# A pooling mixer's running sums in four pieces each, and the memory queries' weights in the mixer's own tiles

## The chip, the cores and the metric

The kernel runs on one core of one Trainium2 chip. A core has a matrix engine (PE, TensorE), three engines that work on vectors (DVE is VectorE, ACT is ScalarE, POOL is GpSimd) and a queue that issues transfers (SP, SyncE). Each engine takes its own instructions strictly in the order in which they stand in its queue, and waits by itself for what an instruction needs. The metric is the device time of one execution in microseconds (us); the time of a kernel is the median of its runs.

## What is computed

The reference is one layer of a hybrid encoder for 1088 tokens (1024 of a prompt and 64 of a sample), width 1024. One normalized input h is projected into the columns of three branches and three gates; the branches are joined by their gates, and a gated feed-forward block follows. Two parts matter here.

```python
h = rmsnorm(x, g_mix)
p = h @ w_in                 # split into qa, ka, va, qi, ki, wi, ub, qm, gates
...
# branch B, the pooling mixer: 4 channel groups of 128 columns of ub,
# for group g the mean of the last 2, 4, 8 or 16 frames, minus the frame,
# then a 128 x 128 map per group and a scale per channel
...
# branch M: the memory queries
qm = rmsnorm(qm.reshape(B, T, N_HEADS_M, HD_M), g_qm)
```

Branch A picks for every query the keys with the highest scores. The kernel finds the cut by halving an integer interval bit by bit, and this search runs through the whole stretch that is looked at here.

## The kernel before, in words

All products are of fp32 values, each held as a rounded high part and the rest (`round_hi`, line 96, on GpSimd here; `lo_of`, line 86, on DVE). `matmul3` (lines 115 to 122) makes three TensorE products of each pair: high by high, high by low, low by high. The normalized input stands transposed in `hh` and `hl`, 8 blocks of 128 rows by 1088 tokens. Tokens are cut into 3 chunks of 364, 362 and 362 columns (`CH`), or into 9 blocks of up to 128 (`TS`).

**The pooling mixer** (pool `pp`) goes over four groups with windows 2, 4, 8 and 16. For each, `wblock` loads 128 columns of weights and splits them into `uhi` and `ulo`; 72 products give the group's 1088 columns; ACT copies them into the tile `e` (lines 470 and 472). GpSimd then makes the running sums (line 485): the first add joins each column with its neighbour, the second adds pairs at distance 2, and so on, so that a window of 2, 4, 8, 16 needs 1, 2, 3, 4 adds, 10 in all, each over up to 1117 columns, into one of the two tiles `pw`. DVE mends the first 16 columns (lines 487 and 488), scales the sum and subtracts the frame (line 489), and ACT and DVE split the result into `ph` and `pl` (line 494 and line 86). `pooled`, the map of a group (9 products, ACT `bh`, DVE `bl`, lines 455 and 456), stands one group later; that of the last group stands in the loop of the memory queries, at block 4.

**The memory queries** (pool `qm`, after the pooling mixer's) load the weights of each half (256 columns) as two pieces of four blocks of 128 rows each, split them into `tmhi` and `tmlo`, make 24 products for each of 9 token blocks (`token_major`), normalize (`head_norm`) and store. The pool `qm` is opened when `pp` is closed and lies in the same place of the on-chip memory, so what is written first there waits for the last readers of the tiles of `pp`.

**What sets the order.** The program is written stage by stage, but a scheduler that simulates a timeline puts each engine's instructions into their final order. So that TensorE has something to do where a stage waits, it puts in products of the gates ("fill work": tile `fl`, ACT's sigmoid `fsg` at line 237, weights `whi` and `wlo` from `fraw`; later also the branches' output products with `fpt`, a load of a stored gate, at line 598, which DVE multiplies in at line 601). The three PSUM buffers of `fl` come free when ACT has made `fsg`.

**The search** runs at the same time on ACT and DVE. In one round, ACT counts for three blocks of queries (line 817, `junk_a`) and DVE for five in four instructions (line 820, `junk_v`), how many scores lie above the candidate. DVE then compares the counts with the cut (`hit_a`, `hit_v`, line 836), sets the bit (`tbit_a`, `tbit_v`, line 837) and makes the next candidate (`cand_a`, `cand_v`, line 834). The next round's counts on ACT wait for `cand_a`, those on DVE for `cand_v`.

Of the kernel before, what the change touches and what calls it, by code (L numbers as in the profile page):

```python
# [9 lines left out]
F32R = mybir.dt.float32r  # L10
AF = mybir.ActivationFunctionType
OP = mybir.AluOpType
# [33 lines left out]
def encoder_step(ctx: ExitStack, tc: tile.TileContext, a: dict, o: list):  # L46
# [38 lines left out]
    def lo_of(lo, src, hi):  # L85
        return V.tensor_tensor(lo, src, hi.bitcast(F32), op=OP.subtract)  # L86
# [70 lines left out]
    def token_major(w, b, n_out):  # L157
        t0, n = TS[b]
        ps = mm()[:n, :n_out]
        matmul3(ps, [(hh[:, k, t0:t0 + n], hl[:, k, t0:t0 + n], w[0][:, k], w[1][:, k]) for k in range(KT)])  # L160
        return ps

    def tm_weights(pool, src, n, bufs=1):
        hi = pool.tile([128, KT, n], F32R, name="tmhi", tag="tmhi", bufs=bufs)
        lo = pool.tile([128, KT, n], F32R, name="tmlo", tag="tmlo", bufs=bufs)
        step = 1024 // n
        for k0 in range(0, KT, step):
            k1 = min(KT, k0 + step)
            raw = wp.tile([128, 1024], F32, name="raw", tag="raw", bufs=3)[:, :(k1 - k0) * n]
            raw = raw.rearrange("p (k j) -> p k j", j=n)  # L170
            SP.dma_start(raw, src[:, k0:k1])
            round_hi(hi[:, k0:k1], raw)
            lo_of(lo[:, k0:k1], raw, hi[:, k0:k1])
        return hi, lo

    def chunks_of(n):
        return [(0, n)] if n <= 512 else [(0, n // 2), (n // 2, n // 2)]
# [215 lines left out]
    with tc.tile_pool(name="mem", bufs=1) as mp:  # L393
        gmem = mp.tile([128, D], F32, name="gmem")
        bcast_row(gmem, a["g_mem"], 0, D)
        gkm = mp.tile([128, 128], F32, name="gkm")
        bcast_row(gkm, a["g_km"], 0, 128)
        mh = mp.tile([128, KT, 256], F32R, name="mh")
        ml = mp.tile([128, KT, 256], F32R, name="ml")
        for i in range(2):  # L400
            xt = raw_tile()
            SP.dma_start(xt, a["mem_prompt"][i * 128:(i + 1) * 128])
            h = row_norm(mp, xt, 128, gmem)
            transpose_split(h, 128, mh[:, :, i * 128:(i + 1) * 128], ml[:, :, i * 128:(i + 1) * 128])
        for c in range(4):
            w = tm_weights(mp, a["w_mem_kv"][c], 256)
            for i in range(2):
                ts = slice(i * 128, (i + 1) * 128)
                ps = mm()[:, :256]
                matmul3(ps, [(mh[:, k, ts], ml[:, k, ts], w[0][:, k], w[1][:, k]) for k in range(KT)])  # L410
                cs = slice((c % 2) * 256, (c % 2) * 256 + 256)
                kv = mp.tile([128, 2, 128], F32, name="kv", tag="kv", bufs=2)
                kf = kv.rearrange("p h d -> p (h d)")
                if c < 2:
                    head_norm(mp, ps, 128, 2, 128, kv)
                    V.tensor_tensor(kv, kv, gkm[:, None, :].to_broadcast([128, 2, 128]), op=OP.mult)
                    SP.dma_start(o[6][ts, cs], kf)
                    SP.dma_start(mem_k[ts, cs], kf)
                else:
                    A.copy(kf, ps)  # L420
                    SP.dma_start(o[7][ts, cs], kf)
                    SP.dma_start(mem_v[ts, cs], kf)
# [6 lines left out]
    if True:  # L429
        W0 = 15 + SEQ + 15  # L430
        E_ = W0 + DEC
        phl_c = tc.tile_pool(name="phl", bufs=1)
        phl = phl_c.__enter__()
        pwh = phl.tile([128, 4, 128], F32R, name="pwh")
        pwl = phl.tile([128, 4, 128], F32R, name="pwl")
        with tc.tile_pool(name="pool", bufs=1) as pp:
            fix = pp.tile([128, 4, 16], F32, name="fix")
            SP.dma_start(fix, bass.AP(tensor=a["fix"].tensor, offset=a["fix"].offset, ap=[[0, 128], [16, 4], [1, 16]]))
            hist = raw_tile()
# [18 lines left out]

            wait = []
            for g, win in enumerate(WINDOWS):  # L460
                wts = [pp.tile([128, 1024], F32R, name=nm, tag=nm, bufs=1) for nm in ("uhi", "ulo")]
                wh, wlo = wblock(a["w_ub"][g], (KT, 128), None, wts)
                e = pp.tile([128, E_], F32, name="e", tag="e", bufs=1)
                V.memset(e[:, 0:15], 0.0)
                G.tensor_scalar(e[:, 15 + SEQ:W0], hc[:, g], 1.0, 1.0, op0=OP.mult, op1=OP.mult)
# [16 lines left out]
                cur, step = e, 1  # L482
                while step < win:
                    nxt = pp.tile([128, E_], F32, name="pw", tag="pw", bufs=2)
                    G.tensor_tensor(nxt[:, 2 * step - 1:], cur[:, 2 * step - 1:], cur[:, step - 1:E_ - step], op=OP.add)
                    cur, step = nxt, 2 * step
                V.tensor_tensor(cur[:, 15:31], cur[:, 15:31], fix[:, g], op=OP.mult)
                V.tensor_tensor(cur[:, 15:31], cur[:, 15:31], e[:, 15:31], op=OP.subtract)
# [8 lines left out]

    with tc.tile_pool(name="qm", bufs=1) as tp:
        for half in range(2):
            w = tm_weights(tp, a["w_qm"][half], 256)  # L500
            for b in range(NB):
                if half == 0 and b == 4:
                    pooled(*wait.pop())
                t0, n = TS[b]
                ps = token_major(w, b, 256)
                qn = tp.tile([128, 2, 128], F32, name="qn", tag="qn", bufs=2)
                head_norm(tp, ps, n, 2, 128, qn[:n])
                SP.dma_start(q_m[t0:t0 + n, half * 256:(half + 1) * 256], qn[:n].rearrange("p h d -> p (h d)"))

    phl_c.__exit__(None, None, None)  # L510


# [998 lines left out]
```

## Time and profile before

| | us |
|---|---|
| median of 3 runs | 1746.39 (1741.99 to 1746.84) |
| the profiled execution's own time | 1744.31 |
| its span, first to last instruction | 1742.5 |
| PE busy with products | 1696.9 (97% of the span) |
| DVE busy | 1178.9 |
| ACT busy | 811.5 |
| POOL busy | 408.5 |

The rows below come from one profiled execution. In a row of a timeline the first number is the start in us from the span's start, the second the time from the first to the last of the instructions joined in it; in brackets, where it stands, is the idle time of the engine just before and what ended it. The granted clock of TensorE is given as a share of its full level.

### The profile page before, as it was taken

How to read it: one execution, taken by the hardware profiler on the slowest of the kernel's cores; microseconds unless marked ns; L12 is line 12 of the kernel's file. 1: busy time of each engine (PE TensorE's matmuls, PEld its weight loads, DVE VectorE, ACT ScalarE, POOL GpSimd, SP SyncE). 2: the span in 40 equal slices, each digit the busy share in tenths (PEclk: the TensorE clock that was granted, in tenths of full speed). 3: DMA queues.
4: the chain of work that ended last, by engine and by line, in shares of the span. 5: the costliest groups of instructions: out<-in, count | busy, mean ns of one | idle time of the engine just before them, and what ended most of it. 6: DMA issues, size and time to landing. Idle time of an engine off the chain costs nothing.

```text
span 1742.5 us, 32497 instructions
## 1 busy us (share of the span) xinstructions
PE 1696.9 (97%) x12088; PEld 1642.4 (94%) x12088; DVE 1178.9 (68%) x2602; ACT 811.5 (47%) x1951; POOL 408.5 (23%) x444
## 2 busy tenths in 40 slices
PE   8999999999999999999999999999999999999999
PEld 7999999899999999877798998999999999999999
DVE  7566999999964443689874688556658656465553
ACT  5457576646632442469732343334434333353431
POOL 4201323345421122675302442000101000000000
PEclk9999999999999999999999999999999999999999
DMA  6122541222366334760273326543445443498661
GB/s 231 59 68 64 170 137 46 80 72 91 118 204 194 99 107 140 259 193 4 77 258 119 112 80 214 177 150 106 174 153 186 142 144 136 133 341 266 208 194 52
DMA packets 147263, 250.86 MB, mean 144 GB/s; under 512 B 16920, under 2 KB 93328, under 8 KB 147104
## 3 DMA queue, kind: packets, MB, share of 16 engines
q1 hardware_dynamic: 147104, 248.78, 43.8%
q8 instruction: 95, 1.56, 0.4%
q14 instruction: 64, 0.52, 0.1%
HBM read 173.63 MB, written 75.09 MB: 143 GB/s over the span
## 4 chain that ended last, share of the span: by engine, by line
PE 59%; DVE 6%; DMA 3%; issue 2%; ACT 2%; POOL 1%; SPq 0%; DVEq 0%; POOLq 0%; ACTq 0%
PE mm L1169 24%; PE mm L1392 13%; PE mm L122 10%; PE fl L122 7%; PE acc L973 1%; DVE lo L86 1%; PE tr L943 1%; PE mm L966 1%; DVE wlo L86 1%; DVE fr L1123 1%; DMA side_a<-gt 1%; DMA gt<-side_m 1%; DVE pl L86 1%; DMA fpt<-gate_b 1%; DMA side_m<-fpt 0%
## 5 line engine op out<-in xcount | busy, mean ns | idle before, releaser
L1169 PE MATMUL mm<-hi,whi 128*128 128x288 f32 (+1 forms) x1120 | 323.0, 289 | 2.3 <-ACT whi L1161 2.3
L1169 PE MATMUL mm<-hi,wlo 128*128 128x288 f32 (+1 forms) x1120 | 323.5, 290 | 0.2
L1169 PE MATMUL mm<-lo,whi 128*128 128x288 f32 (+1 forms) x1120 | 323.4, 289 | 0.0
L1169 PEld LDWEIGHTS mm<-hi,whi 128*128 128x128 f32 x1120 | 211.8, 189 | 3.0 <-ACT whi L1161 3.0
L1169 PEld LDWEIGHTS mm<-lo,whi 128*128 128x128 f32 x1120 | 211.8, 189 | 0.0
L1169 PEld LDWEIGHTS mm<-hi,wlo 128*128 128x128 f32 x1120 | 211.0, 189 | 0.6 <-DVE wlo L86 0.6
L122 PE MATMUL fl<-hh,whi 128*128 128x362 f32 (+1 forms) x576 | 191.1, 332 | 4.5 <-DVE fpt L601 2.3
L122 PE MATMUL fl<-hl,whi 128*128 128x362 f32 (+1 forms) x576 | 190.8, 331 | 0.1
L122 PE MATMUL fl<-hh,wlo 128*128 128x362 f32 (+1 forms) x576 | 188.5, 331 | 0.0
L1392 PE MATMUL mm<-ul,wh 128*128 128x256 f32 (+1 forms) x600 | 171.7, 288 | 0.0
L1392 PE MATMUL mm<-uh,wh 128*128 128x256 f32 (+1 forms) x600 | 171.2, 288 | 0.0
L1392 PE MATMUL mm<-uh,wl 128*128 128x256 f32 (+1 forms) x600 | 170.3, 288 | 0.0
L122 PE MATMUL mm<-tmhi,hh 128*128 128x256 f32 (+3 forms) x432 | 122.2, 288 | 2.7 <-POOL tmhi L96 2.7
L122 PE MATMUL mm<-tmlo,hh 128*128 128x256 f32 (+3 forms) x432 | 123.0, 286 | 0.6 <-DVE tmlo L86 0.6
L122 PE MATMUL mm<-tmhi,hl 128*128 128x256 f32 (+3 forms) x432 | 122.3, 285 | 0.0
L86 DVE TENSOR_TENSOR wlo<-raw,whi 128x1024 fp32r<-128x1024 f32 (+1 forms) x76 | 77.4, 1030 | 58.8 <-ACT whi L1161 38.3
L817 ACT ACTIVATE junk_a<-score,cand_a,sgn_a 128x512 f16<-128x512 f32 (+2 forms) x93 | 95.5, 1027 | 43.3 <-DVE cand_a L834 32.3
L122 PEld LDWEIGHTS fl<-hh,whi 128*128 128x128 f32 x576 | 109.0, 189 | 6.3 <-issue 2.5
L1392 PEld LDWEIGHTS mm<-ul,wh 128*128 128x128 f32 x600 | 112.7, 188 | 0.0
L1392 PEld LDWEIGHTS mm<-uh,wh 128*128 128x128 f32 x600 | 112.4, 188 | 0.0
L1392 PEld LDWEIGHTS mm<-uh,wl 128*128 128x128 f32 x600 | 112.2, 188 | 0.0
L122 PEld LDWEIGHTS fl<-hl,whi 128*128 128x128 f32 x576 | 109.0, 189 | 0.9 <-DVE hl L86 0.4
(404 smaller groups left out, 4565.1 us busy)
## 6 DMA issues: line engine op xcount, KB each, us to landing
uf<-u SPq DMA_DIRECT2D x75, 272.0 KB, 4.5
raw<-in_w_up_dram SPq DMA_DIRECT2D x26, 512.0 KB, 4.0
fraw<-in_w_gates_dram SPq DMA_DIRECT2D x23, 512.0 KB, 3.8
fr<-in_w_gate_dram SPq DMA_DIRECT2D x22, 512.0 KB, 4.3
dr<-in_w_down_dram SPq DMA_DIRECT2D x22, 512.0 KB, 5.8
s<-dr SPq DMA_DIRECT2D x22, 512.0 KB, 3.2
raw<-s SPq DMA_DIRECT2D x44, 256.0 KB, 3.6
side<-side_a SPq DMA_DIRECT2D x8, 1088.0 KB, 7.4
```

The costliest lines, as they stand in the source:

```text
L86: return V.tensor_tensor(lo, src, hi.bitcast(F32), op=OP.subtract)
L122: PE.matmul(ps, l, r, start=i == 0, stop=i == len(prods) - 1)
L817: A.activation(junk[:n, :nk], sc, AF.Sign, bias=bj, scale=1.0 if scale is None else scale[:n, j:j + 1], accum_out=sj)
L943: PE.matmul(lg[:n, i * 512:i * 512 + cn], qT[:, h, :n], kT[:, kv, s, k0 + c:k0 + c + cn], start=s == 0, stop=s == 1)
L966: PE.transpose(pt[:cn, i * n:(i + 1) * n], probs[i][:, c:c + cn], ident[:n, :n])
L973: PE.matmul(acc, vv, r, start=ji == 0 and i == 0, stop=ji == nj - 1 and i == 1)
L1123: V.scalar_tensor_tensor(hb[e][:, :n], ys[i][:, kk], gffn_c[:, kk:kk + 1], rb[:, :n], op0=OP.mult, op1=OP.mult)
L1169: PE.matmul(dst[i], l, r, start=start and j == 0, stop=stop and j == 11, skip_group_check=True)
L1392: PE.matmul(acc[f, i], l[:, fs], r[:, cs], start=start and j == 0, stop=stop and j == 2, skip_group_check=True)
```

## The change

It has two parts.

**The running sums** are cut by columns into pieces of 280 (`PIECE`): four instructions instead of one for each add, 40 instead of 10 on GpSimd. What is computed is the same.

**The weights of the memory queries** no longer go to a pool of their own. The pool `pp` stays open until the memory queries are done. Its two weight tiles `uhi` and `ulo` become two halves of one tile of 2048 columns (tag `ub`). The high part of a half's weights (`qmhi`) takes that tile, and the low part takes the two tiles of the running sums (tag `pw`, 1117 columns each, of which 1024 are used): blocks 0 to 3 in one, blocks 4 to 7 in the other. `token_major` reads the low part as a list of eight blocks. Other callers of `tm_weights` keep `tmhi` and `tmlo`.

```diff
-    def tm_weights(pool, src, n, bufs=1):
-        hi = pool.tile([128, KT, n], F32R, name="tmhi", tag="tmhi", bufs=bufs)
-        lo = pool.tile([128, KT, n], F32R, name="tmlo", tag="tmlo", bufs=bufs)
+    def tm_weights(pool, src, n, given=None):
+        if given:
+            hi, lo = given
+        else:
+            hi, lo = [pool.tile([128, KT, n], F32R, name=nm, tag=nm, bufs=1) for nm in ("tmhi", "tmlo")]
+            lo_all, lo = lo, [lo[:, k] for k in range(KT)]
...
             round_hi(hi[:, k0:k1], raw)
-            lo_of(lo[:, k0:k1], raw, hi[:, k0:k1])
-        return hi, lo
+            if given:
+                lo_of(lo[k0 // step], raw, hi[:, k0:k1])
+            else:
+                lo_of(lo_all[:, k0:k1], raw, hi[:, k0:k1])
+        return hi, [l[:, k] for l in lo for k in range(l.shape[1])] if given else lo
...
-        with tc.tile_pool(name="pool", bufs=1) as pp:
+        pp_c = tc.tile_pool(name="pool", bufs=1)
+        pp = pp_c.__enter__()
+        if True:
+            def ub_tiles():
+                t = pp.tile([128, 2048], F32R, name="ub", tag="ub", bufs=1)
+                return t[:, :1024], t[:, 1024:]
...
-                wts = [pp.tile([128, 1024], F32R, name=nm, tag=nm, bufs=1) for nm in ("uhi", "ulo")]
-                wh, wlo = wblock(a["w_ub"][g], (KT, 128), None, wts)
+                wh, wlo = wblock(a["w_ub"][g], (KT, 128), None, ub_tiles())
...
-                    G.tensor_tensor(nxt[:, 2 * step - 1:], cur[:, 2 * step - 1:], cur[:, step - 1:E_ - step], op=OP.add)
+                    for d0 in range(0, E_, PIECE):
+                        e0, e1 = max(d0, 2 * step - 1), min(d0 + PIECE, E_)
+                        G.tensor_tensor(nxt[:, e0:e1], cur[:, e0:e1], cur[:, e0 - step:e1 - step], op=OP.add)
...
-            w = tm_weights(tp, a["w_qm"][half], 256)
+            given = (pp.tile([128, KT, 256], F32R, name="qmhi", tag="ub", bufs=1),
+                     [pp.tile([128, E_], F32R, name="qmlo", tag="pw", bufs=2)[:, :1024].rearrange("p (k j) -> p k j", j=256)
+                      for _ in range(2)])
+            w = tm_weights(tp, a["w_qm"][half], 256, given)
...
+    pp_c.__exit__(None, None, None)
     phl_c.__exit__(None, None, None)
```

The change moves instructions, since the scheduler sees other waits. TensorE has 12058 products in both. Its order differs only in the stretch from about 245 to 600 us of the trace; from there on the orders are the same. Two places matter.

**GpSimd around the last group of the pooling mixer.** Before, the four adds stand with one weight split between them, and the high parts of the memory queries' weights (`tmhi`) behind all of them:

```order
L465 TENSOR_SCALAR e<-hc 128x15
L485 TENSOR_TENSOR pw<-e 128x1117
L485 TENSOR_TENSOR pw<-pw 128x1115
L485 TENSOR_TENSOR pw<-pw 128x1111
L96 TENSOR_SCALAR whi<-fraw 128x1024
L485 TENSOR_TENSOR pw<-pw 128x1103
L96 TENSOR_SCALAR tmhi<-raw 128x1024 x2
```

After, both pieces of `qmhi` stand behind the first four of the sixteen pieces of the sums:

```order
L477 TENSOR_SCALAR e<-hc 128x15
L499 TENSOR_TENSOR pw<-e 128x279
L499 TENSOR_TENSOR pw<-pw 128x277
L499 TENSOR_TENSOR pw<-e 128x280
L499 TENSOR_TENSOR pw<-pw 128x280
L96 TENSOR_SCALAR qmhi<-raw 128x1024 x2
...
L499 TENSOR_TENSOR pw<-e 128x278
```

So the high part of the weights is ready ahead of most of the sums, and not behind the whole group.

**DVE where the last group ends.** Before, the two low parts `tmlo` stand behind the split `pl` and a round of counts:

```order
L86 TENSOR_TENSOR wlo<-fraw,whi 128x1024
L820 TENSOR_SCALAR junk_v,ssum_v<-score_98,cand_v 128x896
L836 TENSOR_TENSOR hit_v<-ssum_v,cuta_v 128x4
L487 TENSOR_TENSOR pw<-pw,fix 128x16
L489 SCALAR_TENSOR_TENSOR pw<-pw,e 128x1087
...
L86 TENSOR_TENSOR pl<-pw,ph 128x1024
...
L86 TENSOR_TENSOR tmlo<-raw,tmhi 128x1024
```

After, the first low part stands directly behind the scaling of the sums (line 503, line 489 before), the second behind the split:

```order
L838 TENSOR_SCALAR junk_v,ssum_v<-score_98,cand_v 128x896
L503 SCALAR_TENSOR_TENSOR pw<-pw,e 128x1087
L86 TENSOR_TENSOR qmlo<-raw,qmhi 128x1024
L854 TENSOR_TENSOR hit_a<-ssum_a,cuta_a 128x3
L854 TENSOR_TENSOR hit_v<-ssum_v,cuta_v 128x4
L86 TENSOR_TENSOR wlo<-fraw,whi 128x1024
L86 TENSOR_TENSOR pl<-pw,ph 128x1024
L855 SCALAR_TENSOR_TENSOR tbit_a<-hit_a,tbit_a 128x3
L86 TENSOR_TENSOR pl<-pw,ph 128x64
L855 SCALAR_TENSOR_TENSOR tbit_v<-hit_v,tbit_v 128x4
L852 TENSOR_SCALAR cand_a<-tbit_a 128x3
L86 TENSOR_TENSOR qmlo<-raw,qmhi 128x1024
```

The gate's low weights `wlo`, which stood ahead of the scaling, stand behind it.

**TensorE ahead of the memory queries.** Before, 127 fill products (20 ahead of the two transposes of the last group's tail and 107 behind) lie between the map of the third group and the first product with the new weights. Then come only 4 products with `tmhi`, 3 of the last group's map and 7 fills before the first one with `tmlo`:

```order
L122 MATMUL fl<-hh,whi 128x364
L122 MATMUL fl<-hl,whi 128x364
L122 MATMUL fl<-hh,wlo 128x364
L122 MATMUL mm<-tmhi,hh 128x256 x4
L122 MATMUL mm<-ph,pwh 128x364
L122 MATMUL mm<-pl,pwh 128x364
L122 MATMUL mm<-ph,pwl 128x364
```

After, 97 fills lie there (18 and 79). The first 4 products with `qmhi` are strewn among the last 79 (the first of them is the first row below), and behind the fills 92 products of the memory queries follow at once:

```order
L122 MATMUL mm<-qmhi,hh 128x256
L122 MATMUL fl<-hl,whi 128x362
L122 MATMUL fl<-hh,wlo 128x362
L122 MATMUL fl<-hh,whi 128x362
...
L122 MATMUL mm<-qmlo,hh 128x256
L122 MATMUL mm<-qmhi,hl 128x256
```

Of the 92, 29 need only the first low part, and the 30th needs the second. The fills saved here are made later: at the end of the next stage's weights (`w_qa`, `w_kv`), 122 products of the fill work that loads `fpt` are left, where 107 were.

## Rows read from the trace of the kernel before

**Rows 1.** The page's line of busy times over the whole span.

```profile
PE 1696.9 (97%) x12088; PEld 1642.4 (94%) x12088; DVE 1178.9 (68%) x2602; ACT 811.5 (47%) x1951; POOL 408.5 (23%) x444
```

**Rows 2.** Windows: stretch, length, PE, PEld, DVE, ACT, POOL busy, clock, DMA share, GB/s.

```profile
320.00:330.00 10.00, 6.43 (x37) 5.97 (x36) 9.36 (x30) 8.48 (x17) 0.51 (x1) 1.00 0.31 94
330.00:340.00 10.00, 9.41 (x64) 9.41 (x65) 9.71 (x22) 5.59 (x11) 3.52 (x3) 0.83 0.61 176
340.00:350.00 10.00, 10.00 (x84) 10.00 (x84) 9.17 (x36) 9.68 (x33) 2.69 (x7) 1.00 0.16 57
...
540.00:550.00 10.00, 7.66 (x41) 7.43 (x40) 4.07 (x7) 1.33 (x3) 1.05 (x1) 0.83 0.95 310
```

**Rows 3.** Timeline of PE, 301 to 346 us.

```profile
301.71 0.36 PE L122 MATMUL mm<-ph,pwh 128*128 128x364 f32 x1
303.18 0.43 PE L122 MATMUL mm<-pl,pwh 128*128 128x364 f32 x1 [1.11 <-DVE pl L86]
...
321.63 0.44 PE L122 MATMUL fl<-hh,whi 128*128 128x362 f32 x1 [1.48 <-ACT fsg L237]
321.91 0.33 PE L122 MATMUL fl<-hl,whi 128*128 128x362 f32 x1
322.08 0.33 PE L122 MATMUL fl<-hh,wlo 128*128 128x362 f32 x1
...
330.59 1.22 PE L122 MATMUL mm<-tmhi,hh 128*128 128x256 f32 x4 [2.68 <-POOL tmhi L96]
331.61 0.51 PE L122 MATMUL mm<-ph,pwh 128*128 128x364 f32 x1
...
334.14 0.28 PE L122 MATMUL mm<-tmlo,hh 128*128 128x256 f32 x1
...
345.06 0.33 PE L122 MATMUL mm<-ph,pwh 128*128 128x362 f32 x1
```

**Rows 4.** Timeline of POOL, 286 to 332 us.

```profile
288.38 5.03 POOL L485 TENSOR_TENSOR pw<-pw 128x1115 f32<-128x1115 f32 x2
...
307.84 2.05 POOL L485 TENSOR_TENSOR pw<-e 128x1117 f32<-128x1117 f32 x1 [7.67 <-ACT e L472]
309.96 4.17 POOL L485 TENSOR_TENSOR pw<-pw 128x1115 f32<-128x1115 f32 x2
...
315.11 2.56 POOL L485 TENSOR_TENSOR pw<-pw 128x1103 f32<-128x1103 f32 x1
...
329.49 2.06 POOL L96 TENSOR_SCALAR tmhi<-raw 128x1024 fp32r<-128x1024 f32 x2 [11.81 <-issue]
```

**Rows 5.** Timeline of DVE, 287 to 333 us.

```profile
287.00 2.38 DVE L86 TENSOR_TENSOR ulo<-raw,uhi 128x1024 fp32r<-128x1024 f32 x1
...
312.14 2.01 DVE L836 TENSOR_TENSOR hit_a<-ssum_a,cuta_a 128x3 int32<-128x3 f32 x1
...
316.11 1.59 DVE L834 TENSOR_SCALAR cand_a<-tbit_a 128x3 int32<-128x3 int32 x1
...
319.71 0.16 DVE L836 TENSOR_TENSOR hit_v<-ssum_v,cuta_v 128x4 int32<-128x4 f32 x1
...
322.86 1.22 DVE L86 TENSOR_TENSOR wlo<-fraw,whi 128x1024 fp32r<-128x1024 f32 x1
...
325.35 1.28 DVE L489 SCALAR_TENSOR_TENSOR pw<-pw,e 128x1087 f32<-128x1087 f32 x1
...
328.12 1.22 DVE L86 TENSOR_TENSOR pl<-pw,ph 128x1024 fp32r<-128x1024 f32 x1
...
331.24 1.37 DVE L86 TENSOR_TENSOR tmlo<-raw,tmhi 128x1024 fp32r<-128x1024 f32 x1
```

**Rows 6.** Timeline of POOL, short adds elsewhere in the program, 978 to 984 us.

```profile
978.84 0.80 POOL L1081 TENSOR_TENSOR sq<-sq,s 128x288 f32<-128x288 f32 x1 [2.12 <-ACT s L1080]
...
982.02 1.88 POOL L1081 TENSOR_TENSOR sq<-sq,s 128x288 f32<-128x288 f32 x1
```

**Rows 7.** Timeline of PE, the stretch at 544 us.

```profile
544.29 0.41 PE L122 MATMUL fl<-hh,whi 128*128 128x364 f32 x1 [2.34 <-DVE fpt L601]
```

More of the change, by code (lines that the diff above doesn't have):

```diff
@@ L159, in token_major @@
         ps = mm()[:n, :n_out]
-        matmul3(ps, [(hh[:, k, t0:t0 + n], hl[:, k, t0:t0 + n], w[0][:, k], w[1][:, k]) for k in range(KT)])
+        matmul3(ps, [(hh[:, k, t0:t0 + n], hl[:, k, t0:t0 + n], w[0][:, k], w[1][k]) for k in range(KT)])
         return ps
-    def tm_weights(pool, src, n, bufs=1):
-        hi = pool.tile([128, KT, n], F32R, name="tmhi", tag="tmhi", bufs=bufs)
-        lo = pool.tile([128, KT, n], F32R, name="tmlo", tag="tmlo", bufs=bufs)
+    def tm_weights(pool, src, n, given=None):
[4 more added lines that the diff above has]
+            lo_all, lo = lo, [lo[:, k] for k in range(KT)]
         step = 1024 // n
@@ L409, in encoder_step @@
                 ps = mm()[:, :256]
-                matmul3(ps, [(mh[:, k, ts], ml[:, k, ts], w[0][:, k], w[1][:, k]) for k in range(KT)])
+                matmul3(ps, [(mh[:, k, ts], ml[:, k, ts], w[0][:, k], w[1][k]) for k in range(KT)])
                 cs = slice((c % 2) * 256, (c % 2) * 256 + 256)
@@ L431, in encoder_step @@
         E_ = W0 + DEC
+        PIECE = 280
         phl_c = tc.tile_pool(name="phl", bufs=1)
```

## Prediction

> **What bounds the kernel now.** I read the line of busy times first: PE is busy for 97% of the span, and the other engines have room [rows 1]. So what a change off PE can give back is PE's idle time, and what half clock it brings with it. The windows of 10 us show where that is: over the stretch that the change touches, PE is idle for 3.6 us between 320 and 330, and its granted clock falls to 0.83 of full between 330 and 340, while from 340 it is fully busy again [rows 2]. PE's timeline gives the places: 1.11 us for the low part `pl` of the third group, 1.48 us for `fsg`, 2.68 us for `tmhi`, in all 5.27 us [rows 3]. Behind the last of these the clock is low: the four products with `tmhi` take 1.02 us, start to next start (330.59 to 331.61), where 92 such products take 10.92 us from 334.14 to 345.06, or 0.119 us each [rows 3]. [...] I put the loss at 1.4 us. **Ceiling** of what this place can give: 5.3 + 1.4 = 6.7 us.
>
> Why does PE wait there? `tmhi` is made at 329.49, directly when `pl`, started at 328.12 with 1.22 us, ends [rows 4, 5]: it lies where the mixer's tiles lay, and `pl` is their last reader. `pl` follows the scaling at 325.35 [rows 5], which waits its turn on DVE behind a search round. So DVE sets the end of this chain, not GpSimd, whose last add ended at 315.11 + 2.56 = 317.67 [rows 4].
>
> And DVE is late by the adds themselves. A compare of 128x4 takes 0.16 us when nothing disturbs it (319.71), but a `hit_a` of 128x3 took 2.01 and ended at 314.15; the add before it ended at 314.13. A `cand_a` took 1.59 and ended at 317.70; the last add ended at 317.67 [rows 4, 5]. DVE is held until a whole add of GpSimd is over. From the `ulo` at 287.00 (2.38 instead of the 1.22 of `wlo` [rows 5]) to this `cand_a` there are eight such holds, each the excess over the undisturbed duration, in sum 10.4 us (1.2 for the first, 1.4 for the last). While DVE is held, ACT's counts wait too.
>
> [...]
>
> **The change part by part.**
>
> *Shorter adds.* An add of 1117 columns takes 2.05 us [rows 4]; a quarter of it by length is 0.51. The nearest short add is one of 288 columns, 0.80 us undisturbed and 1.88 beside other work [rows 6]. A hold can now last at most one piece: I take 0.6 on average (0.4 if DVE comes in the middle of a piece of 0.8; 0.8 if at its start). Eight holds then cost 4.8 us (3.2 to 6.4) instead of 10.4: 5.6 us saved (4.0 to 7.2). The bound below is that DVE, having got through one hold, is held again by the next piece at its next instruction, so that the number of holds doubles: 16 x 0.6 = 9.6 us, and only 0.8 us are saved. I stay near the single count, since the counts between the compares ran beside adds without being held, and they are most of DVE's time. About 1 us comes from `ulo`, which started 2.2 us after its `uhi` could have let it, behind other DVE work. Together DVE reaches the last scaling some 6.5 us earlier; 1.22 more because `wlo` now stands behind it. 325.35 - 1.22 - 6.5 = **317.6**.
>
> *GpSimd's own time.* Four pieces cost 4 x 0.80 = 3.2 us instead of 2.05, so 10 adds cost some 12 us more over the mixer. This lies beside PE's and DVE's work as long as the last piece ends before 317.6. `e` was complete at about 307.8, when the first add started [rows 4]; with the search rounds of the third group earlier by about 3 us it is complete at 304.5. Twelve pieces then follow at 0.86 (0.80 and a gap): 304.5 + 10.3 = 314.8. That leaves 2.8 us; the cover is gone when a piece takes over 1.1 us.
>
> [...]
>
> *Weights in the mixer's tiles.* `qmhi` waits for the last product of the last group and for its load, not for `pl`; both its pieces stand ahead of twelve of the sums and cost them 2.06 us [rows 4], which the 304.5 above already holds, as the tile is free at 301.71, when the map of the third group starts [rows 3]. The first `qmlo` needs a tile that the last sum has read, so it can follow the scaling at once: 317.6 + 1.28 + 1.22 = 320.1. Then come two compares (0.3), `wlo` (1.2), `pl` (1.2), four small ones (0.6) and the second `qmlo` (1.2) [rows 5]: 320.1 + 4.5 = **324.6**.
>
> *PE.* From 301.71, without the 1.11 wait for `pl` (DVE is earlier by then): 9 products of the map and 97 fills at 0.17 (321.91 to 322.08 [rows 3]; over longer rows 0.167) are 17.7, the two transposes 0.2, four products of `qmhi` 0.5: it reaches the first `qmlo` at 320.1, as it is ready. The 29 products that need this half take 3.4: 323.5. It waits 1.1 us for the second half, and goes on at 324.6. Before, PE stood at 330.59 with 127 fills done and none of these products; 30 fills fewer (5.0 us) and 33 products more (3.9 us) is 1.1 us less work, so the same point was at 329.5. Gain 4.9 us, and 1.4 us more if the clock does not fall, which I expect, as it stayed at full behind the idles of 1.11 and 1.48 us and fell behind 2.68 [rows 2, 3]. `fsg`'s 1.48 us is part of the 4.9: DVE's `cand_a` was what ACT had waited for.
>
> *Behind it.* The program has the same work and, from 600 us, the same order. Search and PE are earlier by about the same, so I expect no new wait from that. The fill work that loads `fpt` stands otherwise between 430 and 600; the place at 544, 2.34 us of idle for `fpt` with DMA at 0.95 and the clock at 0.83 [rows 2, 7], may grow or go. I take nothing for it, plus or minus 2 us.
>
> Sum: 4.9 + 1.4 = 6.3, less 0.3 for small gaps that I can't place: **6 us**.
>
> **The rivals.**
>
> *The holds do not shrink enough.* If every small DVE instruction meets a new piece, 0.8 to 3 us are saved instead of 5.6. With 3, the scaling comes at about 321, the first `qmlo` at 323.5, the second at 328. PE waits 3.4 us at 320.1, and its clock falls as before. Gain 329.5 - 328 = 1.5 us: about 1743 on the profiled execution. For it: the compares, bits and candidates stand in a row without counts between them at a round's end. Against: of the five holds in the last group each had its own DVE instruction and its own instruction on GpSimd, so there is no second instruction that waited behind the same add and could now be caught by its next piece.
>
> *It is given back at 540.* 15 more products with `fpt` are left where the transfers are fullest; five more gates loaded there at 4.7 us each could stretch the idle of 2.34 us and the clock loss to twice that, 3 to 4 us. Gain 2 to 3 us. Against: they are more cover too.
>
> *Slower: DVE holds GpSimd.* The lock goes both ways: an add of 288 columns took 1.88 us where DVE was at work [rows 6]. If the pieces take that, twelve end at 304.5 + 23 = 327.5; DVE's scaling stands first in its queue by then, with the search behind it. The second `qmlo` is ready at 327.5 + 7 = 334.5, against 329.5: 5 us lost, and 2 to 3 more in the third group, where the same happens with eight pieces: 7.5 us slower. It decides from 1.5 us a piece on (304.5 + 12 x 1.5 + 7 = 329.5). Against: of the ten long adds the worst was held by 0.9 us (5.03 for two [rows 4]), and only some pieces can be.
>
> *Nothing happens*: what PE gains ahead of the memory queries it loses within the stretch up to 600, since fills were taken from there. Then 0.
>
> **How the numbers follow.** On the profiled execution (1744.31, of which 1742.5 is span) 6 us give 1738.3. The median of the runs is 2.1 above it: 1746.4 - 6 = **1740.4**. A measurement can tell about 0.3%, or 5.2 us, from no change; the bound of "faster" lies at 1741.2. Chances: the forecast 0.55, holds 0.2, given back 0.1, nothing 0.07, slower 0.08. In the forecast's own range, 3.5 to 9 us, a fifth or so lies within 0.3%; a few of "given back" may still be faster. So faster 0.47, same 0.45, slower 0.08. Range: the forecast's upper end of gain 9 gives 1737.4, and 1 us for the median's own scatter 1736.4; the other end takes in the holds and "nothing": 1746.8. Only "slower" and the tails are left out.
>
> **What would show it.** Right: in the changed kernel's trace the compares and candidates beside the pieces take under 1 us; the pieces take 0.5 to 0.9; the last scaling starts near 317.6 and the first product with `qmlo` near 320; PE's idle between 301 and 335 is under 2.5 us and its clock stays at full there. Wrong: pieces over 1.5 us, the scaling waiting for GpSimd instead of a search round, an idle before `qmlo` of over 2.5 us with the clock at half behind it, or a new idle between 430 and 600 larger than the 2.34 us at 544.

## The result, and the profile after

The changed kernel takes 1737.16 us (median of 6 runs, 1734.27 to 1739.12) against 1745.95 us for the kernel before (6 runs); the ratio is 0.9949, with a 95% interval of 0.9936 to 0.9962. That is 8.8 us faster, or 6.6 to 11.2. The forecast was 6 us, 1740.4 in a range of 1736.4 to 1746.8. The profiled executions differ by less: 1744.31 before, 1739.12 after (spans 1742.5 and 1737.2, so 5.3 us); that of after is the slowest of its six.

The windows of the profile after (columns as in [rows 2]) show the place that the forecast spoke of, and another one that it did not:

```profile
320.00:330.00 10.00, 9.80 (x83) 9.60 (x82) 9.46 (x29) 6.57 (x20) 0.90 (x2) 1.00 0.54 177
330.00:340.00 10.00, 10.00 (x78) 10.00 (x77) 9.45 (x35) 8.39 (x24) 2.66 (x6) 1.00 0.17 55
...
470.00:480.00 10.00, 6.63 (x26) 6.61 (x27) 10.00 (x27) 1.28 (x4) 3.52 (x4) 0.66 0.48 146
...
540.00:550.00 10.00, 9.40 (x60) 9.05 (x61) 5.83 (x13) 3.63 (x12) 0.95 (x3) 1.00 1.01 332
```

Between 320 and 340 PE is idle for 0.2 us instead of 4.2 (3.57 and 0.59 [rows 2]), and its clock stays at full, where it was 0.83. Between 470 and 480 it is idle for 3.4 us at a clock of 0.66. These are PE's idles of the timeline after at the places in question (start, length, engine, line, tile; in brackets the idle before):

```profile
319.69 0.39 PE L122 MATMUL mm<-qmlo,hh 128*128 128x256 f32 x1 [0.24 <-DVE qmlo L86]
...
323.59 0.39 PE L122 MATMUL mm<-qmlo,hh 128*128 128x256 f32 x1 [0.20 <-DVE qmlo L86]
...
473.37 0.67 PE L122 MATMUL fl<-bh,whi 128*128 128x362 f32 x1 [4.53 <-DVE fpt L619]
...
540.13 0.41 PE L122 MATMUL fl<-hh,whi 128*128 128x364 f32 x1 [1.76 <-DVE fpt L619]
```

The three idles of 1.11, 1.48 and 2.68 us [rows 3] became two of 0.24 and 0.20. DVE's timeline beside it, with the compares next to the sums, the scaling and the two low parts:

```profile
301.29 1.03 DVE L852 TENSOR_SCALAR cand_a<-tbit_a 128x3 int32<-128x3 int32 x1
...
311.46 0.79 DVE L854 TENSOR_TENSOR hit_a<-ssum_a,cuta_a 128x3 int32<-128x3 f32 x1
...
312.29 0.71 DVE L855 SCALAR_TENSOR_TENSOR tbit_a<-hit_a,tbit_a 128x3 int32<-128x3 int32 x1
...
317.21 1.29 DVE L503 SCALAR_TENSOR_TENSOR pw<-pw,e 128x1087 f32<-128x1087 f32 x1
318.42 1.22 DVE L86 TENSOR_TENSOR qmlo<-raw,qmhi 128x1024 fp32r<-128x1024 f32 x1
...
322.31 1.22 DVE L86 TENSOR_TENSOR qmlo<-raw,qmhi 128x1024 fp32r<-128x1024 f32 x1
```

The scaling starts at 317.21, where it started at 325.35 [rows 5]. And GpSimd's timeline:

```profile
301.23 2.08 POOL L96 TENSOR_SCALAR qmhi<-raw 128x1024 fp32r<-128x1024 f32 x2 [0.20 <-PE mm L122]
304.85 1.26 POOL L499 TENSOR_TENSOR pw<-e 128x280 f32<-128x280 f32 x2 [1.54 <-ACT e L482]
306.07 6.91 POOL L499 TENSOR_TENSOR pw<-pw 128x280 f32<-128x280 f32 x10
```

Twelve pieces run from 304.85 to 312.98, at 0.68 us each, gaps included.

To follow the gain through the program I use a **lead**. TensorE makes the same products in all these kernels (each trace has 12088 TensorE instructions), in another order. Each product counts with its undisturbed time from start to start (0.167 us for 362 or 364 columns, 0.119 for 256, from [rows 3]), added up from 200 us on; the lead of a kernel at a time of before is how much earlier it has done the same sum. It is worked out from PE's timelines, is good to about half a microsecond as arithmetic, and compares two single executions, which scatter by more (up to 1.6 us, last section). For the changed kernel it is 0.2 us at 301 us of before's time, 1.7 at 312, 2.9 at 324, 6.7 at 338, 7.0 at 398, 7.3 at 460; then 3.4 at 493, and 5.0 from 559 to the end. So some 7 us are won ahead of the memory queries, 4 are lost near 470, and 1.6 are won at 541. What is left at the end, 5.0 us, is about what the two profiled executions differ by (5.3 us of span); the remaining 3.5 us of the 8.8 between the medians stand in no trace.

### The profile page after: what moved, and what is told of

Read it like the earlier page. It is cut to its first block, busy times and chain, and to the rows that moved or that the text cites. A ratio compares the mean times of both kernels' runs of the same rounds, so it can differ in the third digit from the quotient of the medians.

```text
span 1737.2 us, 32520 instructions
## 1 busy us (share of the span) xinstructions
PE 1694.2 (98%) x12088; PEld 1641.7 (95%) x12088; DVE 1173.9 (68%) x2602; ACT 810.1 (47%) x1951; POOL 417.7 (24%) x474
## 4 chain that ended last, share of the span: by engine, by line
PE 61%; DVE 6%; DMA 3%; issue 3%; POOL 2%; ACT 1%; SPq 1%; POOLq 0%; DVEq 0%; ACTq 0%
PE mm L1187 24%; PE mm L1410 13%; PE mm L122 12%; PE fl L122 7%; PE acc L991 1%; PE tr L961 1%; DVE lo L86 1%; DMA side_m<-fpt 1%; DVE wlo L86 1%; PE mm L984 1%; DVE fr L1141 1%; DMA side_a<-gt 1%; POOL pr L971 1%; POOL sm L969 1%; DMA gt<-side_m 0%
## 5 line engine op out<-in xcount | busy, mean ns | idle before, releaser
L122 PEld LDWEIGHTS fl<-hh,wlo 128*128 128x128 f32 x576 | 107.9, 188 | 0.6
L86 DVE TENSOR_TENSOR wl<-raw,wh 128x512 fp32r<-128x512 f32 x75 | 51.8, 690 | 71.0 <-ACT wh L1400 70.9
L838 DVE TENSOR_SCALAR_CACHE_REDUCE junk_v<-score,cand_v 64x192 f16<-64x192 f32 (+1 forms) x124 | 94.0, 758 | 2.6
```

The source lines that it names most:

```text
L122: PE.matmul(ps, l, r, start=i == 0, stop=i == len(prods) - 1)
L838: V.tensor_scalar(junk[:n, :nk], sc, bj, None, op0=OP.is_ge, op1=OP.add, accum_out=sj)
```

## The experiments

Leads, as defined above, in us at a time of before's trace; the last column is the median of the runs minus the median of before in the same job.

| kernel | 338 | 398 | 460 | 493 | 623 | runs |
|---|---|---|---|---|---|---|
| the change | 6.7 | 7.0 | 7.3 | 3.4 | 5.1 | -8.8 |
| the change once more | 6.1 | 6.3 | 6.7 | 3.4 | 6.4 | -7.3 |
| pieces of 280 alone | 6.6 | 6.9 | 3.7 | 3.6 | 1.2 | -2.5 |
| placement alone | 1.1 | 1.4 | -0.7 | -0.4 | 2.1 | -2.5 |
| change, pieces of 560 | 2.1 | 2.5 | 1.0 | 0.8 | 1.7 | -5.8 |
| change, pieces of 200 | 7.5 | 8.0 | 6.6 | 4.7 | 6.7 | -7.3 |
| change, pieces of 140 | 7.6 | 8.1 | 6.9 | 9.1 | 12.3 | -14.7 |
| the same once more | 7.6 | 8.0 | 7.0 | 10.4 | 13.0 | -14.1 |
| change, pieces of 94 | 7.6 | 7.8 | 7.2 | 8.0 | 8.6 | -9.7 |
| pieces of 140 alone | 8.0 | 7.6 | 5.9 | 3.4 | 3.1 | -3.6 |
| change, each piece twice | 0.6 | 0.7 | -2.1 | 1.7 | 5.8 | -6.4 |
| change, two tables, one `kt` | 7.7 | 8.2 | 5.3 | 4.8 | 5.3 | -4.7 |
| change, two tables | 5.1 | 4.8 | 1.3 | 0.8 | -1.2 | -4.4 |

**The change once more.**

> The changed kernel once more. Theory: the gain made ahead of the memory queries (about 7 us of TensorE progress at 335 us) repeats in every execution, and the wait of some 4.5 us near 470 us, with half clock behind it, is part of the instruction order: idle 3 to 5 us there again, 5 to 9 us faster than before in all. Rival: the wait near 470 us is an accident of transfers in the one profiled execution; then its idle is under 1.5 us this time and the profiled execution is 8 to 11 us faster than before's.

Measured: 1738.97 us against 1746.30 (ratio 0.9960, 0.9948 to 0.9972). The lead at 338 us is 6.1, and the idle near 470 us is there again, 3.69 us, with the clock at 0.66 from 470 to 480:

```profile
474.35 0.67 PE L122 MATMUL fl<-bh,whi 128*128 128x362 f32 x1 [3.69 <-DVE fpt L619]
...
470.00:480.00 10.00, 6.30 (x24) 6.01 (x24) 9.23 (x25) 1.28 (x4) 4.50 (x6) 0.66 0.36 109
```

So both the gain and the loss belong to the instruction order, and neither to one execution.

**The pieces alone.**

```diff
+        PIECE = 280
...
-                    G.tensor_tensor(nxt[:, 2 * step - 1:], cur[:, 2 * step - 1:], cur[:, step - 1:E_ - step], op=OP.add)
+                    for d0 in range(0, E_, PIECE):
+                        e0, e1 = max(d0, 2 * step - 1), min(d0 + PIECE, E_)
+                        G.tensor_tensor(nxt[:, e0:e1], cur[:, e0:e1], cur[:, e0 - step:e1 - step], op=OP.add)
```

> Only the running sums in pieces of 280 columns; the memory queries' weights stay in a pool of their own. Theory (DVE is held by whole adds): the compares beside the sums take under 1 us and the last scaling comes near 319 us, some 6 us earlier than before, so that tmhi can start near 323; TensorE reaches it after 98 fills near 322.5 and waits 1 to 2.5 us, and has gained 4 to 6 us at 340 us. Rival (the placement does it): tmhi still waits for the split of the last group, TensorE idles over 4 us there, and the gain at 340 us is under 2 us.

Measured: 1743.78 us (ratio 0.9982, 0.9970 to 0.9994). The lead at 338 us is 6.6, all that the whole change has there, and more than the 4 to 6 expected. The scaling, the split `pl` (two instructions in the second row), and the weights, on DVE, GpSimd and PE:

```profile
315.70 1.29 DVE L492 SCALAR_TENSOR_TENSOR pw<-pw,e 128x1087 f32<-128x1087 f32 x1
...
319.25 1.35 DVE L86 TENSOR_TENSOR pl<-pw,ph 128x1024 fp32r<-128x1024 f32 x2
...
320.75 2.07 POOL L96 TENSOR_SCALAR tmhi<-raw 128x1024 fp32r<-128x1024 f32 x2 [7.37 <-issue]
...
324.13 0.38 PE L122 MATMUL mm<-tmlo,hh 128*128 128x256 f32 x1 [0.37 <-DVE tmlo L86]
```

`tmhi` still follows the end of `pl` (319.25 + 1.35 = 320.60) after 0.15 us, as before (329.49 [rows 4]), but 8.7 us earlier. TensorE waits 0.37 us. Neither the idle of 1 to 2.5 us that the theory expected here came nor the rival's of over 4: the scaling was 3 us earlier than I had said. The lead is lost later: 3 us near 427 us, where PE waits 1.97 us for `tmlo` of the next stage, and again near 543 us (4.50 us for `fpt`).

**The placement alone.**

```diff
-                    for d0 in range(0, E_, PIECE):
-                        e0, e1 = max(d0, 2 * step - 1), min(d0 + PIECE, E_)
-                        G.tensor_tensor(nxt[:, e0:e1], cur[:, e0:e1], cur[:, e0 - step:e1 - step], op=OP.add)
+                    G.tensor_tensor(nxt[:, 2 * step - 1:], cur[:, 2 * step - 1:], cur[:, step - 1:E_ - step], op=OP.add)
```

> Only the placement of the memory queries' weights in the mixer's tiles; the ten sums are whole adds. Theory (the holds set DVE's pace): the compares beside the sums take 1 to 2 us as before, the scaling comes near 324 us, the first low part near 326.5, the second near 331; TensorE, with about 110 fills ahead, is ready near 322.5, waits over 3 us in sum and loses clock; gain at 340 us between -1 and 2 us. Rival (the placement does it): TensorE waits under 1 us ahead of the memory queries and has gained 5 us or more at 340 us.

Measured: 1743.81 us (ratio 0.9986, 0.9976 to 0.9995); lead at 338 us 1.1. DVE's timeline has the long holds again, with the scaling at 322.94, and PE waits for the map's result `bl`, which stands behind a hold:

```profile
287.54 2.01 DVE L852 TENSOR_TENSOR hit_a<-ssum_a,cuta_a 128x3 int32<-128x3 f32 x1
...
309.96 2.01 DVE L853 SCALAR_TENSOR_TENSOR tbit_a<-hit_a,tbit_a 128x3 int32<-128x3 int32 x1
...
322.94 1.28 DVE L501 SCALAR_TENSOR_TENSOR pw<-pw,e 128x1087 f32<-128x1087 f32 x1
...
312.73 0.39 PE L122 MATMUL mm<-qmhi,hh 128*128 128x256 f32 x1 [2.20 <-DVE bl L469]
```

Where the waits were expected (for the two low parts) there are none over 0.4 us, as TensorE was late by the 2.20 us and two shorter idles before; the size of the lead came as the theory said, its place did not. From these two kernels: ahead of the memory queries the pieces bring nearly all. What the placement brings, 1.1 us by itself and 0.1 on top, is less than two executions of one order can differ by, so it is not told from nothing.

**The size of the pieces.** One number is changed, `PIECE = 280` into 560, 140 (run in two jobs), 200 or 94.

> The changed kernel with pieces of 560 columns, two per add. Theory (a hold lasts as long as what is left of the running GpSimd instruction): a piece takes about 1.1 us, the compares beside the sums up to 1.2, and the last scaling comes some 2 us later than with 280 columns; progress of TensorE at 340 us 3 to 5.5 us ahead of before's. Rival (any cutting is enough, because the scheduler sees shorter steps): 6.5 us or more, as with 280.

> The changed kernel with pieces of 140 columns, eight per add. From 0.65 us at 280 columns and 2.05 at 1117 a piece of 140 should take 0.41 us (0.18 fixed, 1.67 ns a column). Theory: holds shrink to 0.4 or less, DVE reaches the last scaling up to 1 us earlier than with 280, and since TensorE there waits only 0.2 to 0.4 us for it, the progress at 340 us stays at 6.5 to 7.5 us. Rival (GpSimd's instruction count costs): 16 more instructions per add chain delay the last sum beyond the scaling's turn, DVE waits for GpSimd, and the progress falls under 5.5 us.

> The kernel with pieces of 140 columns once more, to hold its gain against the chance of one job. Theory (its better end comes from its own instruction order behind 440 us, which is fixed): 13 to 16 us below before, idle ahead of fpt near 475 us under 1.5 us, lead at 560 us 11 to 13 us. Rival (scatter between jobs): 7 to 10 us below before, like 280 columns.

> Pieces of 200 columns, six per add, weights placed as in the change. Theory (the size of the pieces acts only ahead of the memory queries, and what follows behind 440 us is the accident of the order that the scheduler finds): lead at 400 us 6 to 8 us, between those of 280 (6.4 to 7.0) and 140 (8.0); behind 480 us anything between 0 and 12 us. Rival (finer pieces themselves bring the later gain): lead at 560 us between 5 and 12, in step with the size, about 9 us.

> Pieces of 94 columns, twelve per add, weights placed as in the change. From the measured sizes a piece takes 0.18 + 94 x 1.67 ns = 0.34 us, so an add 4.1 us against 2.05 whole. Theory: lead at 400 us 6 to 8 us, no better than 140, as TensorE hardly waits there any more and the last sum comes later; the lead at 560 us is not in step with the size. Rival (finer is better throughout): lead over 8.5 us at 400 and over 12.5 at 560 us.

Measured: 560: 1741.07 us (ratio 0.9968, 0.9957 to 0.9978). 140: 1732.17 us (0.9914, 0.9899 to 0.9929) and 1730.67 us (0.9905, 0.9888 to 0.9922). 200: 1737.46 us (0.9944, 0.9927 to 0.9961). 94: 1735.04 us (0.9935, 0.9914 to 0.9957). The kernel with 140 columns beats both kernels.

Groups of GpSimd's pieces from 240 to 345 us (instruction, count, then busy us and mean ns, then idle before). With 280 columns:

```profile
L499 POOL TENSOR_TENSOR pw<-pw 128x280 f32<-128x280 f32 x12 | 9.0, 762 | 0.2
L499 POOL TENSOR_TENSOR pw<-pw 128x277 f32<-128x277 f32 x3 | 1.9, 649 | 0.5 <-DVE cand_a L852 0.3
```

With 140 columns:

```profile
L499 POOL TENSOR_TENSOR pw<-pw 128x140 f32<-128x140 f32 x36 | 15.5, 457 | 0.0
L499 POOL TENSOR_TENSOR pw<-pw 128x137 f32<-128x137 f32 x3 | 1.2, 413 | 0.0
```

With 94 columns:

```profile
L499 POOL TENSOR_TENSOR pw<-pw 128x94 f32<-128x94 f32 x60 | 20.2, 371 | 0.0
L499 POOL TENSOR_TENSOR pw<-pw 128x84 f32<-128x84 f32 x6 | 2.0, 336 | 0.0
```

A piece beside little other work takes 0.65 us at 277 columns, 0.41 at 137 and 0.34 at 84; with 2.05 us at 1117 [rows 4] that is a line of 0.18 us and 1.67 ns a column. The lead at 398 us is 2.5, 7.0, 8.0, 8.1 and 7.8 us for 560, 280, 200, 140 and 94 columns: it grows until TensorE no longer waits there, and then it stays. Only the step from 560 to 280 is clear of the scatter between executions. With 560 seven of the compares, bits and candidates take 0.98 to 1.31 us, the scaling comes at 323.48, 6.3 us later than with 280 and not the 2 expected, and PE has idles of 1.22, 0.95 and 1.60 us between 272 and 313 us for `bl` and the group's low weights; this is less of a lead than I had expected (3 to 5.5). Its profiled execution was the slowest of its ten (1746.82 us), so its leads stand for a slow one.

Behind 440 us the size does not settle the gain alone. From 560 to 140 columns the lead at 623 us does grow (1.7, 5.1 to 6.4, 6.7, 12.3 to 13.0), but with 94 it is 8.6, and with 140 in the pieces alone 3.1. That the instruction order decides is the likely reading (the change and 140 columns were each profiled twice with the same order, and come out alike), and no run changes the order alone. What the better end of 140 is made of the windows show, the change first and then 140:

```profile
445.00:500.00 55.00, 49.93 (x347) 49.28 (x347) 47.07 (x143) 20.91 (x82) 18.34 (x26) 0.94 0.53 160
...
445.00:500.00 55.00, 53.97 (x397) 53.30 (x396) 47.27 (x153) 23.28 (x95) 22.99 (x29) 1.00 0.56 162
```

From 445 to 620 us PE is idle for 1.8 us with 140 columns (1.4 in the second job), and its clock is at 1.00 from 445 to 500 us and from 540 to 550; in the change it is idle for 7.3 us (5.0 in its second execution), and before for 4.7. The first expectation for 140 speaks of the lead alone: the drop of 14 us was not foreseen, and the second job bears it out. With 140 the idle near 470 us is short:

```profile
475.46 0.43 PE L122 MATMUL fl<-bh,whi 128*128 128x362 f32 x1 [1.00 <-DVE fpt L619]
```

and that at 544 us (2.34 us [rows 7]) is one of 0.75 us for another load. With 200 the idle near 470 is 3.41 us, with 94 it is 1.15, and with 94 there are 1.99 us at 536.

**The pieces of 140 columns alone.** The pieces kernel above, with 140 for 280.

> Pieces of 140 columns with the memory queries' weights in their own pool, as before. Theory (the pieces bring the lead, and the placement adds under 1 us to it): lead at 340 to 400 us 6 to 8 us. Rival (with the finer pieces the placement is what counts): under 4 us there. Behind 440 us either way the order decides.

Measured: 1741.20 us (ratio 0.9976, 0.9962 to 0.9990). The lead at 338 us is 8.0, as much as with the placement (7.6) within what the lead is good to. It falls by 2 near 424 us and by some 3 near 475 (an idle of 3.45 us for `fpt`). So here too the pieces bring the lead, and what is left of it hangs on the order behind.

**Each piece made twice.**

```diff
-                        G.tensor_tensor(nxt[:, e0:e1], cur[:, e0:e1], cur[:, e0 - step:e1 - step], op=OP.add)
+                        for _ in range(2):
+                            G.tensor_tensor(nxt[:, e0:e1], cur[:, e0:e1], cur[:, e0 - step:e1 - step], op=OP.add)
```

> The changed kernel with each piece of the sums made twice (the same values again), so 80 instead of 40 instructions, at 0.65 us each. It stands for pieces that take twice as long. Theory (GpSimd has about 4 us of slack behind the last piece, 313.0 against the scaling at 317.2): the last twelve pieces become 24 and end near 321 us; the scaling comes then and not with its search round, DVE is held more often, and the progress at 345 us falls from 6.9 to between -1 and 3.5 us. Rival (GpSimd is off the path): progress of 6 us or more.

Measured: 1740.51 us (ratio 0.9968, 0.9957 to 0.9979); the lead at 338 us is 0.6, and it stays there to 410 us. But the way is not the one expected. The scheduler put 144 fill products ahead instead of 59 in the last stretch before the memory queries, so TensorE did not wait for the scaling at all, though this came at 340.69 us; a weight split in GpSimd's queue waited 6.19 us for its load, ahead of eight pieces:

```profile
329.80 1.05 POOL L96 TENSOR_SCALAR whi<-fraw 128x1024 fp32r<-128x1024 f32 x1 [6.19 <-DMA fraw<-in_w_gates_dram]
330.81 6.92 POOL L500 TENSOR_TENSOR pw<-pw 128x265 f32<-128x265 f32 x8
```

The lead is missing because TensorE waited 1.12 and 2.91 us for `bl` at 291 and 318 us. So more work on GpSimd does cost the lead, through DVE; whether by 4 us of slack, as the theory had it, this run doesn't tell. That its whole time is nevertheless 6.4 us below before's is due to the stretch behind 440 us, which is another in this order too.

**Two buffers for the rotary tables.** The wait near 470 us is for `fpt` by the trace. Its chain, followed back through the queues of SP, GpSimd and DVE in the changed kernel:

```profile
462.12 0.65 SPq L536 DMA_DIRECT2D cosa<-in_cos_a_dram  x1
...
467.67 1.43 POOL L546 TENSOR_TENSOR cosa<-cosa,g 128x576 f32<-128x576 f32 x1 [3.44 <-DMA cosa<-in_cos_a_dram]
469.05 0.71 POOL L126 TENSOR_TENSOR hr<-hr,mhalf 128x2 f32<-128x2 f32 x1
...
469.79 0.29 DVE L216 TENSOR_TENSOR qn<-mm,hr 128x128 f32<-128x128 f32 x1 [3.65 <-POOL hr L126]
470.00 2.60 DVE L893 TENSOR_SCALAR score<-score,rank_a 128x512 f32<-128x512 f32 x3
...
472.79 0.52 DVE L619 SCALAR_TENSOR_TENSOR fpt<-fpt,fl 128x362 f32<-128x362 f32 x1
```

The table `cosa` of the queries has one buffer; the table of the keys can be loaded only when the last block of queries has been turned by it. GpSimd waits for the load with the root `hr` behind, DVE waits for `hr` with `qn` at the head of its queue, and the gating of `fpt`, on which the PSUM buffers of the fill work wait, stands behind. In the first of two kernels the tables get two buffers each and the tile `kt` one; in the second `kt` keeps its two, and the two gain rows go to a staging tile.

```diff
-        cosa = qp.tile([128, NB, HDA], F32, name="cosa")
-        sina = qp.tile([128, NB, HDA], F32, name="sina")
...
+            cosa = qp.tile([128, NB, HDA], F32, name="cosa", tag="cosa", bufs=2)
+            sina = qp.tile([128, NB, HDA], F32, name="sina", tag="sina", bufs=2)
...
+            return cosa, sina
```

> The changed kernel with two buffers for each of the two rotary tables, so that the keys' tables can be loaded and multiplied while the queries' are still read (the tile kt has one buffer instead of two, to make room). Up to the query stage the order is that of the changed kernel. Theory: the wait near 470 us comes from the table's load, which can't start before the last query block has read the old table, and from the products on DVE that stand behind it; with two buffers its idle is under 1 us, the clock stays at full, and the time is 3 to 5 us below the changed kernel's. Rival: the wait comes from somewhere else (DVE's own work, the load of fpt), and the idle of 3 us or more stays within 450 to 490 us, with the time within 1.5 us of the changed kernel's.

> The changed kernel with two buffers for each rotary table as before, this time with kt left at two buffers; the room comes from the two gain rows, which go to a staging tile. Theory: the wait near 470 us for fpt, which stands behind the keys' table, is gone (no idle over 1 us between 440 and 480 us), the lead of about 7 us holds until 500 us, and the time is 2 to 4 us below the changed kernel's. Rival (the fill work ahead of 550 us is the limit, as transfers fill the lines there): the idle moves to the stretch from 480 to 550 us, and the time is within 1.5 us of the changed kernel's.

Measured: 1741.63 us (ratio 0.9973, 0.9963 to 0.9984) and 1742.52 us (0.9974, 0.9965 to 0.9984). The wait for `fpt` near 470 us is gone in both: no idle for it between 440 and 480 us. So the table is what the wait hangs on. How long it lasts hangs on the transfers too: the load of the keys' `cosa` takes 2.9 us before and 5.4 us in the change (the last number, in us), with DMA at 0.80 from 462 to 468 us; in the change's second execution it is 4.6 us.

```profile
cosa<-in_cos_a_dram SPq DMA_DIRECT2D x1, 288.0 KB, 2.9
...
cosa<-in_cos_a_dram SPq DMA_DIRECT2D x1, 288.0 KB, 5.4
```

In the first, TensorE's order is the changed kernel's up to 475 us, past the wait. But both kernels are slower than the change, against the 3 to 5 us and 2 to 4 us gained that the theory expected (in one job the first took 1741.63 us and the change 1738.97). In the first kernel PE waits elsewhere:

```profile
409.74 0.39 PE L122 MATMUL mm<-tmhi,hh 128*128 128x256 f32 x1 [2.08 <-DVE qn L216]
...
480.02 0.53 PE L571 MATMUL mm<-ident_r,kd 128*128 128x128 f32 x3 [1.94 <-DVE kd L565]
```

and three idles of 1.13, 0.47 and 1.41 us for `fpt` stand between 533 and 541. The second has four idles of 0.9 to 1.8 us from 396 to 482 us, and three for `fpt`, 4.2 us together, between 535 and 544. The fill work that had waited at 470 is moved to where it waits as well. That the transfers are the limit there, as the rival says, is not shown: the edit changes the order of every engine from somewhere in the query stages on (in the second kernel GpSimd's already from 327 us), so more than the table's wait is different.

What nearly all the kernels with one buffer show is the wait itself: before, the change (two executions), pieces, placement, 560, 200, 94, 140 alone and 140 (first job) stand 1.30, 4.53, 3.69, 2.02, 3.11, 2.38, 3.41, 1.15, 3.45 and 1.00 us there for `fpt`; 140 in its second job has no idle over 0.4 us, with the same order as in the first, and the kernel with each piece twice has none behind its own load of the keys' table (494 us).

## Why the prediction was right

The direction, the size within its range, and the mechanism ahead of the memory queries held. That the total came so near is in part luck: of some 7 us won there 4 were lost behind, which the prediction put at nothing, and 1.6 came back. Point by point:

**The holds.** DVE was held until GpSimd's instruction was over (the `tbit_a` of 312.29 ends at 313.00, the last piece at 312.98): forecast eight holds of 0.6 us, 4.8 us in all. From the first piece of the third group (282.39 us) to the scaling I count, of over 0.1 us, nine holds by pieces, 3.8 us in sum (0.2 to 0.6 each; the `hit_a` of 0.79 us above is the longest), and two by splits of weights, 0.9 and 0.8 us (the first is the `cand_a` of 1.03 us at 301.29). Before it was eight and 10.4 us, one of them, of 0.6 us, by a split. So the sum is near, 5.5 us against 4.8 (3.2 to 6.4), but by more and shorter holds than said. The argument that no second instruction would be caught by the next piece did not hold: the `hit_a` at 311.46 and the `tbit_a` at 312.29 were held one behind the other. The `cand_a`, a TENSOR_SCALAR that reads one tile only, was held as well, before (1.59 us [rows 5]) and after (1.03 us at 301.29). That DVE is held and until when, the rows show; by what it is held, no run shows.

**The scaling** at 317.6: measured 317.21, and 318.99 in the second execution. The first low part at 320.1: 319.64. The second at 324.6: 323.53. **TensorE** at the first low part at 320.1: 319.69, with 0.24 us of idle; the wait of 1.1 us for the second was 0.20. No clock was lost (1.00 from 300 to 340 us); but the reason given, by the lengths of the idles, does not hold in other runs (last section). The 1.4 us that the sum takes for the clock are borne out by the trace of before: the 14 products from 330.59 to 334.14 us take 3.55 us from start to start, where by the undisturbed 0.119 and 0.167 us they take 2.15, at these granted clocks (columns as in [rows 2]):

```profile
330.00:332.00 2.00, 1.41 (x6) 1.41 (x7) 1.96 (x5) 1.78 (x4) 2.00 (x3) 0.53 0.24 81
332.00:334.00 2.00, 2.00 (x10) 2.00 (x9) 2.00 (x4) 0.57 (x1) 1.52 (x1) 0.62 0.41 117
334.00:336.00 2.00, 2.00 (x18) 2.00 (x18) 2.00 (x5) 0.00 (x0) 0.00 (x0) 1.00 0.86 254
```

The gain there, forecast 6.3, is a lead of 6.7 (6.1 in the second execution).

**GpSimd.** The last piece at 314.8: measured 312.98. I took 0.86 us for a piece, by the short adds elsewhere [rows 6]; it is 0.68. The price of one more instruction is 0.18 us by the line through the sizes. The ten adds took 22.7 us before and the forty pieces 32.1: 9.4 more, where the prediction took 12.

**The credit.** The prediction costed both parts as one chain, with the placement as what lets the low parts follow the scaling at once, and did not ask what the pieces do alone. They alone give 6.6 us where the change has 6.7, since an early scaling makes an early `pl`, and so frees the tiles of the mixer early. The placement alone gives 1.1.

**Behind it.** "I expect no new wait" was wrong, and "plus or minus 2 us" too small: 4 us were lost at 470, and 1.6 came back at 541. The 4.53 us at 473 are larger than the 2.34 at 544: this is one of the signs that the prediction named for being wrong, and it came. Before, the wait stands in small, in a row that the prediction does not show:

```profile
483.84 0.43 PE L122 MATMUL fl<-bh,whi 128*128 128x362 f32 x1 [1.30 <-DVE fpt L601]
```

The sum over the program was near the forecast because these partly cancel. The rival that the gain is given back named the right tile, `fpt`, but the wrong place, and as cause the loads of `fpt` where transfers are full; what stood in the way was the load of the keys' table, itself slower than before (5.4 us against 2.9). The slower rival (pieces of 1.88 us) came for five pieces of the forty, which took 1.19 to 2.04 us, and none of them stands among the last twelve.

**What stays open**: which feature of the order makes the lead change behind 460 us, by anything from -2.8 us (140 alone) to +7.9 (each piece twice) up to 623 us. Thirteen traces give leads there from -1.2 to 13.0, and no part of the change sets them in step.

## What to carry to other kernels

If VectorE and GpSimd work side by side, look at the small VectorE instructions, not at the busy shares: a compare of 0.16 us took 2.01 here and ended with a GpSimd add, and cutting the adds cost 0.18 us a cut and brought TensorE 7 us ahead, of which 5 were left at the end. Before a tile is moved to free a pool earlier, ask whether the chain that frees it can be made shorter; that was worth more than the move (a lead of 6.6 us against 1.1 at 338 us). And where a scheduler places the fill work, a gain in one stretch is a new order in the next: measure several settings of the same idea and keep the best, since 140 columns gave twice what 280 did, with the same lead where the pieces act.

## What the runs showed of the hardware

In these runs the length of TensorE's idle alone does not tell whether the granted clock falls behind it. Idles of 1.97 us (the pieces alone, 427 us) and of 2.20 us (the placement alone, 313 us) were followed by a window with a granted clock of 0.50 of full; behind one of 2.08 us at 410 us in the first kernel with two tables the clock stayed at 1.00, and so it did around a longer one for `fpt`, of 3.41 us (200 columns, 474 us). In windows of 2 us, pieces alone:

```profile
426.00:428.00 2.00, 1.22 (x5) 1.22 (x6) 2.00 (x5) 0.82 (x3) 1.59 (x1) 0.70 0.19 27
428.00:430.00 2.00, 2.00 (x12) 2.00 (x11) 2.00 (x8) 1.97 (x4) 0.00 (x0) 0.50 0.83 256
```

the placement alone:

```profile
314.00:316.00 2.00, 2.00 (x9) 2.00 (x9) 1.93 (x6) 2.00 (x5) 0.08 (x1) 0.50 0.19 61
```

and the kernel with two tables:

```profile
408.00:410.00 2.00, 0.26 (x2) 0.27 (x3) 2.00 (x8) 1.79 (x13) 1.74 (x4) 1.00 0.00 0
410.00:412.00 2.00, 2.00 (x19) 2.00 (x19) 2.00 (x8) 2.00 (x9) 0.59 (x1) 1.00 0.00 0
```

And 200 columns, with the idle and its window of 10 us:

```profile
473.96 0.43 PE L122 MATMUL fl<-bh,whi 128*128 128x362 f32 x1 [3.41 <-DVE fpt L619]
...
470.00:480.00 10.00, 6.09 (x37) 5.50 (x36) 8.80 (x25) 0.67 (x2) 6.03 (x5) 1.00 0.54 165
```

So a term for the clock, in this kernel, belongs to a place and its rows, and can't be taken over from an idle of the same length.

Executions of one order differ by up to 1.6 us at 338 us already: TensorE's order up to there is the same in the change, its second run and the two kernels with two tables, with leads of 6.7, 6.1, 7.7 and 5.1 us at 338 us; in the last GpSimd's order is another from 327 us on.
